# A ring of four buffers for the wide sums of w_ada, and the scan tables' products behind the last h

## The chip, the cores and the metric

The kernel runs on one core of a Trainium2 chip. The metric is the device time of one execution in microseconds, as the median of several runs. Five engines work side by side, each with an instruction queue of its own that it takes in order: TensorE (PE; its weight loads are the profile's PEld), VectorE (DVE), ScalarE (ACT), GpSimd (POOL) and SyncE (SP), which here issues most transfers between HBM and on-chip memory. They wait for one another by semaphores.

## What is computed

One decoder block on 256 positions of width 2048, in float32. A conditioning vector c makes six vectors of scales and shifts through `w_ada` (2048 x 12288, 100 MB). The normalised input, scaled by `sc1` and shifted by `sh1`, is h; h times `w_in` gives the input u of a state-space branch, q, k, v of an attention branch and two gates. A merge, an output projection and an MLP of width 8192 follow. Cut to what matters here:

```python
c_act = jax.nn.silu(c)
mod = c_act @ w_ada[l] + b_ada[l]
sh1, sc1, g1, sh2, sc2, g2 = [m[:, None, :] for m in jnp.split(mod, N_MOD, axis=-1)]
h = rms_norm(x, norm_mix_g[l]) * (1.0 + sc1) + sh1
proj = h @ w_in[l]
u, q, k, v, ga, gb = jnp.split(proj, split_at, axis=-1)
y_ssm = s5_branch(u, ssm_a_re[l], ssm_a_im[l], ssm_log_dt[l], ...)
y_att = moba_attention(q.reshape(shp), k.reshape(shp), v.reshape(shp), rel_bias)
merged = (jax.nn.sigmoid(ga) * (y_ssm @ w_proj_ssm[l])
          + jax.nn.sigmoid(gb) * (y_att @ w_proj_attn[l]))
x = x + g1 * (merged @ w_out[l])
h2 = rms_norm(x, norm_mlp_g[l]) * (1.0 + sc2) + sh2
x = x + g2 * (jnp.square(jax.nn.relu(h2 @ w_ff1[l])) @ w_ff2[l])
```

## The kernel before

**Weight tiles.** Every matrix is read in tiles of 128 rows by 1024 columns (0.5 MB). `load` (L157) puts the transfer on SP's queue, into one of seven buffers `wraw`. `split` makes two halves for the matmuls: ScalarE casts the tile to the high part `whi` (L162), VectorE subtracts that from the tile for the low part `wlo` (L164); each has four buffers. Every product is high x high, high x low and low x high. `gemm_t` (L222 to L224) takes the weights as the stationary operand, in 24 matmuls of 256 columns a tile; `gemm_n` (L275 to L279) takes h as the stationary one, in 12 matmuls of 512 columns.

**The units of w_in.** h comes into being piece by piece, 128 rows ("k tile", kt 0 to 15) or two of them at a time. So the product with `w_in` is cut into units (which, first group, last group): `which` is 0 q, 1 k, 2 v, 3 u, 4 one gate, and the k tiles come in groups of 1, 3, 4 and 8 (kt 0; 1 to 3; 4 to 7; 8 to 15). `qkvu` runs a unit, starts the stream of the next one (`prime`) and moves the sums out of PSUM. Numbered through, unit (0,1,2) has weight tiles 18 to 24, then (1,2,2), (2,2,2), (3,2,2) have four each, (4,2,3) has 37 to 48 (kt 4 to 15), (0,3,3) has 49 to 56, (3,3,3) 57 to 64, (1,3,3) 65 to 72 and (2,3,3) 73 to 80.

**The sums of w_ada.** The first two vectors of `w_ada` (`sc1`, `sh1`) are needed for h. For kt 0 to 3 TensorE sums them (`ada_first`). For kt 4 to 15 VectorE does, in 24 wide sums: `ada_wide` loads 128 rows of 2048 columns (1 MB, two transfers, L375) and multiplies them with silu(c) in one instruction with a running sum (L381). Four sums make two k tiles of h: `hjob` lets ScalarE scale and shift (L514) and splits the result (L162, L164 on `ah`). The buffers of the wide sums lie in `hv` and `hq`, the slots that `bp` ("VT") and `cc` ("QT") of the state-space tables take over later. `ringed` sets which load follows which sum: for the first twelve sums there are four buffers, load i + 4 after sum i; for the last twelve (kt 10 to 15) two buffers, those of `hq`, load i + 2 after sum i.

**Lanes.** Work beside the units is dispatched by lanes: after each weight tile `step` adds a lane's rate to its credit (at most 3) and runs one job for each whole credit. A job's instructions get their place in the program there; a planner with a timeline of its own then sets the order on each engine by priority (weight tiles rank higher by an offset) and dependency.

- Lane `ada`: three empty jobs, the first four loads, two empty jobs, then the 24 sums and 6 `hjob`s, then 97 late jobs (the sums of the other vectors, half as wide, L339). Its rate is R1 = .92; from `hjob(8)` (tile 23) R2; from `hjob(14)` R3 = .15; from the flush on R4 = .5, later rates from 1.0 to .1. So `hjob(14)`, 15 jobs behind `hjob(8)`, would come at .56 on tile 50; `want` (L1139) runs the lane as far as the k tile of the moment needs it, and forces it on tile 47, where kt 14 begins.
- Lane `ssm`: eighteen empty jobs, then the tables of the scan: `ssm_build1` in four parts of six products on VectorE (L676 to L678; the first part into `cmp`, the others into `bp`), `ssm_cc`, `ssm_build3`, transposes on TensorE (`ssm_build2`, L711) and `ssm_build4` (matmuls L748, sums L754), which reads `tt` in slot "T". Rate 1.0, SR1 after unit (0,1,2), SR2 = 1.4 from `hjob(14)`. By the count, five jobs of `ssm_build1` are dispatched ahead of `hjob(14)`.

**After (3,3,3).** `hop_in` copies u into the scan's layout in 32 small transfers on POOL's queue (L853). `flush("ssm")` dispatches what is left of that lane, the `ada` lane goes to R4, `bias_load` loads the attention's bias `tz` into slot "T" in four transfers on POOL's queue (L550), and units (1,3,3) and (2,3,3) follow. Then one gate runs with the attention's jobs (`attn1`, L801 to L813, reads `tz` on VectorE) beside it, and after that the scan.

Of the kernel before, what the change touches and what calls it, by code (L numbers as in the profile page):

```python
# [39 lines left out]
OFF = 300  # L40
HOT = 4000
OF1 = 3000
SR1 = .27
SR2 = 1.4
SC = 1.0
NS = 2
SL = 18
R1 = .92
R2 = .56
R3 = .15  # L50
R4 = .5
RS0 = 1.0
# [25 lines left out]
class Kern:  # L78
# [872 lines left out]
    def body(self):  # L951
# [121 lines left out]
        def seeds(which):  # L1073
            def f(b):
                d, view = views(which, b)
                return lambda o: (view(o), d)
            return [f(b) for b in range(4)]
# [3 lines left out]
        def evac(which, banks, add):  # L1081
            if which == 4 and add:
                self.ga = self.slot("X16", [P, 2, D], name="ga")
            elif which == 4:
                gpart["p"] = self.slot("S4", [P, 2, 1024], name="gp")
            for b in range(4):
                d, view = views(which, b)
                if which == 4 and add:
                    d = self.ga[:, b // 2, (b % 2) * 512:(b % 2) * 512 + 512]
                nc.scalar.copy(d, view(banks[b]))  # L1090
# [23 lines left out]
        def place(which, g0, g1):  # L1114
            return win, range(groups[g0][0], sum(groups[g1])), (1024, 2048, 3072, 0, 4096)[which]

        def qkvu(u, after=None):
            which, g0, g1 = u
            f = self.gemm_n if which in (2, 4) else self.gemm_t
            banks = f(*place(*u), self.ah, self.al, seed=seeds(which) if g0 else None)  # L1120
            if after:
                self.prime(*place(*after))
            evac(which, banks, g0)
# [3 lines left out]
        def hjob(k0):  # L1127
            def f():
# [3 lines left out]
                if k0 == 8:  # L1132
                    self.lanes["ada"][1] = R2
                if k0 == 14:
# [9 lines left out]
        nop = lambda: None  # L1144
        units = []
        wide = [h[:, 2 * i:2 * i + 2, :].rearrange("p k c -> p (k c)") for h in (hv, hq) for i in range(2)]
        ring = wide * 3 + wide[2:4] * 6
        for k0 in range(4, KT, 2):
            units += mod1(k0, 2, ring) + [(None, hjob(k0))]
        free = {None: range(4)}  # L1150
        free.update({i: (i + 4,) for i in range(8)})
        free.update({i: (i + 2,) for i in range(10, 22)})

        def drain(n):
            while len(ready) < n:
# [10 lines left out]
        for u, after in zip(order, order[1:] + [None]):  # L1166
            qkvu(u, after)
            if u == (0, 1, 2):
                self.lanes["ssm"][1] = SR1
        self.want = lambda kt: None  # L1170
        self.hop_in()
        self.flush("ssm")
        self.lanes["ada"][1] = R4
        self.bias_load()
        qkvu((1, 3, 3), (2, 3, 3))
        qkvu((2, 3, 3))
        ga = self.ga
        self.asc = ga[:, :, 1024:1792]
# [389 lines left out]
```

## Time and profile before

| | |
|---|---|
| three runs, median (lowest to highest) | 1390.79 us (1390.17 to 1392.34) |
| the profiled execution | 1391.66 us |
| its span, first to last instruction | 1389.9 us |
| granted clock of TensorE, mean | 0.992 |
| read from HBM | 350.79 MB |
| busy: TensorE, VectorE, ScalarE, GpSimd | 97%, 75%, 55%, 3% |

The profile shows one execution. A time in it counts from the span's first instruction. Rows of the order of time have the start, the duration, the engine, the line, the operation, the tile written and the tiles read; in square brackets stands how long the engine had been idle before, and what ended that. Rows of groups have the number of instructions, the busy time and the mean duration in ns, then the idle time in front of them. "SPq" and "POOL DMA" rows are the issue of a transfer, not the transfer. TensorE's matmuls overlap, so their spacing, not their duration, is the pace.

### The profile page before, as it was taken

The page shows a single profiled execution, that of the slowest core. Times are in us where ns is not written, and L with a number is a line of the kernel's source. Part 1 is how long each engine was busy: PE and PEld are TensorE (multiplying, and loading weights), DVE is VectorE, ACT ScalarE, POOL GpSimd, SP SyncE. Part 2 cuts the span into 40 slices and gives each one's busy share as a digit, 9 for nine tenths or more (in the row PEclk, how much of TensorE's full clock was granted, in tenths as well). Part 3 has the DMA queues.
Part 4 walks back from the last instruction along what each step waited for, and adds up shares of the span by engine and source line. Part 5 has one row for each costly group of instructions (what it writes and reads, how often), then busy time and mean ns, then how long its engine had stood idle before and what let it go on. Part 6 is the DMA issues. An engine that isn't in the chain of part 4 may idle for free.

```text
span 1389.9 us, 21608 instructions
## 1 busy us (share of the span) xinstructions
PE 1354.8 (97%) x8314; PEld 1173.4 (84%) x8314; DVE 1045.5 (75%) x1449; ACT 758.2 (55%) x1052; POOL 42.6 (3%) x96
## 2 busy tenths in 40 slices
PE   7999899999999999999999999999999999999997
PEld 5898789988788897888999888888888888888885
DVE  6798987688797898988885976777666555555676
ACT  6767458456655843446555665444453554634543
POOL 1000001300002200000000000000000000000000
PEclk9999989999999999999999999999999999999999
DMA  9999946898355989898597878798867656566562
GB/s 374 407 396 382 349 150 203 242 326 322 107 172 192 329 291 332 292 387 303 204 355 231 297 242 251 246 255 283 256 232 248 198 188 197 182 193 195 177 199 69
DMA packets 112424, 356.43 MB, mean 256 GB/s; under 512 B 12241, under 2 KB 12273, under 8 KB 111905
## 3 DMA queue, kind: packets, MB, share of 16 engines
q1 hardware_dynamic: 109280, 348.96, 73.0%
q0 software_dynamic: 2896, 5.83, 1.5%
q8 instruction: 65, 1.06, 0.3%
q10 hardware_dynamic: 144, 0.26, 0.1%
q14 instruction: 39, 0.31, 0.1%
HBM read 350.79 MB, written 2.51 MB: 254 GB/s over the span
## 4 chain that ended last, share of the span: by engine, by line
PE 83%; DVE 7%; ACT 4%; DMA 3%; issue 2%; SPq 0%; ACTq 0%; DVEq 0%
PE pn L275 15%; PE pn L277 15%; PE pn L279 15%; PE pd L240 13%; PE pd L244 7%; PE pt L224 5%; PE pt L222 5%; PE pt L223 5%; DVE wlo L164 2%; ACT whi L162 1%; DMA wraw<-in_w_proj_ssm_dram 1%; DVE ahm L381 1%; DVE wraw L339 1%; DMA ahm<-in_wat_dram 1%; PE rk L748 1%
## 5 line engine op out<-in xcount | busy, mean ns | idle before, releaser
L162 ACT CAST whi<-wraw 128x1024 fp32r<-128x1024 f32 x448 | 467.4, 1052 | 511.8 <-PE pn L277 224.7
L164 DVE TENSOR_TENSOR wlo<-wraw,whi 128x1024 fp32r<-128x1024 f32 x448 | 545.0, 1222 | 258.8 <-ACT whi L162 254.6
L240 PE MATMUL pd<-h2h,whi 128*128 128x512 f32 x800 | 208.8, 393 | 0.0
L275 PE MATMUL pn<-whi,ff 128*128 128x512 f32 x496 | 193.0, 389 | 0.0
L277 PE MATMUL pn<-whi,ff 128*128 128x512 f32 x496 | 193.0, 389 | 0.0
L279 PE MATMUL pn<-wlo,ff 128*128 128x512 f32 x496 | 191.6, 389 | 0.0
L240 PEld LDWEIGHTS pd<-h2h,whi 128*128 128x128 f32 x800 | 140.6, 189 | 21.8
L339 DVE SCALAR_TENSOR_TENSOR wraw<-wraw,cb 128x1024 f32<-128x1024 f32 x128 | 155.9, 1218 | 0.0
L275 PE MATMUL pn<-whi,ah 128*128 128x512 f32 x320 | 126.8, 402 | 3.4 <-ACT ah L162 1.5
L277 PE MATMUL pn<-whi,ah 128*128 128x512 f32 x320 | 126.6, 396 | 0.0
L244 PEld LDWEIGHTS pd<-h2h,wlo 128*128 128x128 f32 x800 | 116.0, 190 | 12.4
L244 PE MATMUL pd<-h2h,wlo 128*128 128x256 f32 x800 | 119.2, 282 | 0.0
L279 PE MATMUL pn<-wlo,ah 128*128 128x512 f32 x320 | 117.4, 400 | 0.4 <-DVE wlo L164 0.4
L222 PE MATMUL pt<-ah,whi 128*128 128x256 f32 x384 | 108.9, 290 | 4.3 <-ACT ah L162 3.5
L224 PE MATMUL pt<-ah,wlo 128*128 128x256 f32 x384 | 103.4, 287 | 7.3 <-DVE wlo L164 7.2
L279 PEld LDWEIGHTS pn<-wlo,ff 128*128 128x128 f32 x496 | 93.1, 188 | 19.5
L275 PEld LDWEIGHTS pn<-whi,ff 128*128 128x128 f32 x496 | 93.1, 188 | 19.1
L277 PEld LDWEIGHTS pn<-whi,ff 128*128 128x128 f32 x496 | 93.2, 188 | 19.0
L223 PE MATMUL pt<-ah,whi 128*128 128x256 f32 x384 | 107.8, 285 | 0.0
L222 PEld LDWEIGHTS pt<-ah,whi 128*128 128x128 f32 x384 | 73.8, 193 | 6.5 <-ACT ah L162 3.6
L224 PEld LDWEIGHTS pt<-ah,wlo 128*128 128x128 f32 x384 | 71.7, 194 | 8.2 <-DVE wlo L164 8.1
L275 PEld LDWEIGHTS pn<-whi,ah 128*128 128x128 f32 x320 | 61.0, 191 | 17.6 <-ACT ah L162 2.0
(376 smaller groups left out, 2029.3 us busy)
## 6 DMA issues: line engine op xcount, KB each, us to landing
wraw<-in_w_ff_dram SPq DMA_DIRECT2D x256, 512.0 KB, 4.8
wraw<-in_w_in_dram SPq DMA_DIRECT2D x128, 512.0 KB, 5.9
wraw<-in_wat_dram SPq DMA_DIRECT2D x128, 512.0 KB, 5.7
ahm<-in_wat_dram SPq DMA_DIRECT2D x48, 512.0 KB, 9.9
wraw<-in_w_out_dram SPq DMA_DIRECT2D x32, 512.0 KB, 6.6
wraw<-in_w_proj_attn_dram SPq DMA_DIRECT2D x16, 512.0 KB, 5.8
wraw<-in_w_proj_ssm_dram SPq DMA_DIRECT2D x16, 512.0 KB, 6.5
ahm<-in_wan_dram SPq DMA_DIRECT2D x8, 512.0 KB, 11.4
```

The source lines that it names most:

```text
L162: h = self.nc.scalar.copy(hi, src)
L164: s = self.nc.vector.tensor_sub(lo, src, hi.bitcast(F32))
L222: nc.tensor.matmul(o, hi[:, c], xh[:, kx, :], start=st, stop=False, skip_group_check=True)
L223: nc.tensor.matmul(o, hi[:, c], xl[:, kx, :], start=False, stop=False, skip_group_check=True)
L224: self.mm = nc.tensor.matmul(o, lo[:, c], xh[:, kx, :], start=False, stop=sp, skip_group_check=True)
L240: nc.tensor.matmul(banks[blk], hi[:, cut(blk, k)], x2[:, ks[k], :, :], start=i + k == 0, stop=False, skip_group_check=True)
L244: self.mm = nc.tensor.matmul(banks[blk][:, S:2 * S], lo[:, cut(blk, k)], x2[:, ks[k], 0, :], start=False, stop=last and k == 1, skip_group ...
L275: nc.tensor.matmul(o, xh[:, kx, tk], hi[:, c], start=q == 0 and not full, stop=False, skip_group_check=full)
L277: nc.tensor.matmul(o, xl[:, kx, tk], hi[:, c], start=False, stop=False, skip_group_check=full)
L279: self.mm = last = nc.tensor.matmul(o, xh[:, kx, tk], lo[:, c], start=False, stop=q == n - 1, skip_group_check=full)
L339: v.scalar_tensor_tensor(w, w, 1.0, self.cb[:, (i % 2) * 1024:(i % 2 + 1) * 1024], op0=OP.mult, op1=OP.mult, accum_out=pc[:, i:i + 1])
L381: sm = v.scalar_tensor_tensor(w, w, 1.0, self.cb, op0=OP.mult, op1=OP.mult, accum_out=pc[:, i:i + 1])
```

## The change

Three constants and three places of the order of work. The last twelve wide sums use the same four buffers as the first twelve, load i + 4 after sum i. The `ada` lane runs at .75 jobs a weight tile instead of .56 between `hjob(8)` and `hjob(14)`: by the count, the last wide sum is dispatched on tile 42 and `hjob(14)` on tile 43. The `ssm` lane has rate 0 after unit (0,1,2), so the first `ssm_build1` is dispatched with `hjob(14)`; the last job of the lane falls on tile 65 (it fell on 64). Unit (1,3,3) is moved ahead of `flush("ssm")`, the change to R4 and `bias_load`; its tiles are run with R3, and ten late jobs by the end of (2,3,3) become eight.

```diff
-SR1 = .27
+SR1 = 0.0
...
-R2 = .56
+R2 = .75
...
-        ring = wide * 3 + wide[2:4] * 6
+        ring = wide * 6
...
-        free.update({i: (i + 4,) for i in range(8)})
-        free.update({i: (i + 2,) for i in range(10, 22)})
+        free.update({i: (i + 4,) for i in range(20)})
...
         self.hop_in()
+        qkvu((1, 3, 3), (2, 3, 3))
         self.flush("ssm")
         self.lanes["ada"][1] = R4
         self.bias_load()
-        qkvu((1, 3, 3), (2, 3, 3))
         qkvu((2, 3, 3))
```

## The prediction

> **What bounds the kernel now.** I read the page first, then stretches of the span (the view of windows), then the order of time on TensorE, VectorE and the queues inside the one stretch that stands out.
>
> ```profile
> PE 1354.8 (97%) x8314; PEld 1173.4 (84%) x8314; DVE 1045.5 (75%) x1449; ACT 758.2 (55%) x1052; POOL 42.6 (3%) x96
> ...
> PE   7999899999999999999999999999999999999997
> ...
> PEclk9999989999999999999999999999999999999999
> ```
>
> PE is busy 97% of the span, so an edit can win only where PE stands idle or runs at a lowered clock. The slices show that at the start and the end, which the change doesn't touch, and in the fifth and sixth slices (139 to 208 us), where both rows have an 8. The windows narrow this down; their columns are the stretch, its length, the busy time of each engine, the granted clock, the DMA share and GB/s.
>
> ```profile
> 0.00:100.00 100.00, 87.77 (x766) 77.44 (x766) 76.99 (x177) 70.94 (x113) 4.40 (x19) 0.98 1.00 395
> 100.00:154.00 54.00, 53.08 (x336) 47.66 (x337) 49.44 (x56) 37.29 (x57) 1.31 (x2) 1.00 1.00 366
> 154.00:168.30 14.30, 14.30 (x65) 11.84 (x64) 12.95 (x16) 6.81 (x9) 0.00 (x0) 1.00 1.00 382
> 168.30:175.40 7.10, 0.32 (x3) 0.12 (x1) 5.11 (x7) 0.94 (x1) 0.00 (x0) 0.87 0.61 231
> 175.40:183.80 8.40, 7.78 (x22) 6.34 (x23) 6.39 (x11) 2.94 (x6) 0.00 (x0) 0.50 0.38 125
> 183.80:231.00 47.20, 47.20 (x387) 46.66 (x386) 41.72 (x41) 37.51 (x68) 0.00 (x0) 1.00 0.56 176
> 231.00:340.00 109.00, 109.00 (x823) 95.94 (x823) 84.05 (x134) 60.17 (x103) 17.26 (x36) 1.00 0.87 296
> 340.00:360.00 20.00, 17.41 (x113) 13.69 (x113) 7.75 (x17) 16.11 (x36) 0.11 (x1) 0.91 0.23 79
> ```
>
> From 168.3 to 175.4 PE does nothing, and up to 183.8 it runs at half the clock. Until 168.3 the DMA engines are full (share 1.00); in the hole they are not. PE in order of time:
>
> ```profile
> 168.22 0.28 PE L222 MATMUL pt<-ah,whi 128*128 128x256 f32 x1
> 168.34 0.28 PE L223 MATMUL pt<-ah,whi 128*128 128x256 f32 x1
> 175.48 0.58 PE L224 MATMUL pt<-ah,wlo 128*128 128x256 f32 x1 [6.86 <-DVE wlo L164]
> ```
>
> PE wants the low half of a weight tile (`wlo`), which VectorE has not made yet. VectorE in the same time:
>
> ```profile
> 161.55 2.28 DVE L381 SCALAR_TENSOR_TENSOR ahm<-ahm,cb 128x2048 f32<-128x2048 f32 x1
> ...
> 171.99 2.29 DVE L381 SCALAR_TENSOR_TENSOR ahm<-ahm,cb 128x2048 f32<-128x2048 f32 x1 [1.99 <-DMA ahm<-in_wat_dram]
> 174.21 0.08 DVE L381 DVE_READ_ACCUMULATOR ahm<-ahm,cb 128x1 f32 x1
> 174.21 2.35 DVE L164 TENSOR_TENSOR wlo<-wraw,whi 128x1024 fp32r<-128x1024 f32 x2
> 176.48 0.15 DVE L990 TENSOR_TENSOR B<-pw,cols 128x2 f32<-128x2 f32 x1
> 178.50 0.69 DVE L164 TENSOR_TENSOR ah<-htmp,ah 128x512 fp32r<-128x512 f32 x1 [1.87 <-ACT ah L162]
> ```
>
> The last wide sum stands in VectorE's queue ahead of that low half and waits for its own load; the last h (k tiles 14 and 15) follows, complete at 178.50 + 0.69 = 179.2, and the remaining tiles of unit (4,2,3) had to wait for it. On SP's queue that load was issued late:
>
> ```profile
> 163.87 0.81 SPq L375 DMA_DIRECT2D ahm<-in_wat_dram  x2
> ```
>
> It went out in the moment in which the sum two places before it had ended (161.55 + 2.28 = 163.8): a ring of two buffers. It landed when the sum could begin, at 171.9, eight microseconds later. So the bound here is the ring, then VectorE's order, then PE.
>
> **The stall's price.** These are PE's groups between 168.35 and 183.8:
>
> ```profile
> L279 PE MATMUL pn<-wlo,ah 128*128 128x512 f32 x5 | 2.9, 573 | 0.0
> L277 PE MATMUL pn<-whi,ah 128*128 128x512 f32 x4 | 2.5, 628 | 0.0
> L275 PE MATMUL pn<-whi,ah 128*128 128x512 f32 x4 | 2.1, 669 | 0.5 <-ACT ah L162 0.5
> L224 PE MATMUL pt<-ah,wlo 128*128 128x256 f32 x4 | 1.8, 457 | 6.9 <-DVE wlo L164 6.9
> L223 PE MATMUL pt<-ah,whi 128*128 128x256 f32 x4 | 1.5, 382 | 0.0
> L222 PE MATMUL pt<-ah,whi 128*128 128x256 f32 x4 | 1.5, 381 | 0.0
> ```
>
> One L279 and one L222 of these began before the stretch, which leaves 12 matmuls of 512 columns and 11 of 256. At the full clock a 512-wide one follows the last after 0.227 us (the window from 154 to 168.3 has 63 starts of them in its 14.3 us), a 256-wide one after 0.12 (168.22 to 168.34 above). That is 12 x 0.227 + 11 x 0.12 = 4.0 us of work in 15.5 us: **11.5 us lost**, 7.1 by standing still, 4.4 by the half clock and a short gap before 178.52. This is all that the change can win here; below, it can win nothing.
>
> **Ring and rate.** Counted from the lanes, the last sum is dispatched on weight tile 42 in place of 47, and the last h on 43 in place of 47 (where `want` forces it). PE reaches tile 47 at 168.3. Is h ready by then? Three counts. By bytes: the last load stands behind 24 wide loads (25.2 MB), 16 pieces of the first sums (8.4), 42 weight tiles (22.0), x, the scan's tables and small ones (3.7): 59.3 MB. The windows show 39.5 MB by 100 us and 19.8 more by 154, together 59.3. The queue had moved as many bytes at 154; only their order changes. Sum 2.3, then 4.9 us from the sum's end to h (174.28 to 179.2): **h at about 161**. By VectorE's work:
>
> ```profile
> L164 DVE TENSOR_TENSOR wlo<-wraw,whi 128x1024 fp32r<-128x1024 f32 x26 | 30.8, 1216 | 0.0
> L381 DVE SCALAR_TENSOR_TENSOR ahm<-ahm,cb 128x2048 f32<-128x2048 f32 x12 | 27.4, 2284 | 4.3 <-DMA ahm<-in_wat_dram 4.3
> ...
> L676 DVE TENSOR_TENSOR tt<-cmp,AB 128x512 f32<-128x512 f32 x2 | 1.3, 681 | 0.0
> ```
>
> (groups of VectorE from 100 to 170 us). From in front of h go ten products of 0.68 (the first table's six and four of the next: 6.8 us), waits for wide loads (4.3 in these rows and the 1.99 at 171.99) and four low halves of 1.2 (4.8), since h stands four tiles earlier: 17.9 us, so again 161. By PE: that is 7 us ahead of need. I take the stall as gone, -11.5; the other end is 0.
>
> What may be late next is VectorE before 168, where the sums are now packed closer: twelve from tile 25 to 42. PE takes 2.88 us for a transposed tile (24 x 0.12) and 2.72 for a straight one, 50 us for these 18. VectorE's part is 18 x 1.2 + 12 x 2.3 + three splits of 0.69 and small ones, about 52.
>
> ```profile
> 105.50:168.30 62.80, 62.22 (x361) 54.55 (x360) 56.89 (x64) 41.80 (x62) 0.75 (x2) 1.00 1.00 371
> ```
>
> Over the whole stretch it fits: 56.9 - 6.8 (products) + 5.3 (two sums and a split that came after 168.3) = 55.4 of 62.8. But in the bunch it is 2 us over, with the lead of a few low halves as cover. Bounds 0 and +4 (twice that excess); I take +0.5.
>
> A rule of the Trainium skill speaks against the ring: the page "DMA: Bandwidth & Descriptors", section "Specifications", puts the limit of one core's HBM traffic at about 358 GB/s (further down it has 425 measured for one core streaming alone). By it the 59.3 MB alone would need 166 us, an estimate that would put h near 173 and leave most of the stall. The row from 0 to 100 us has 395 GB/s, so the measurement decides against the rule here, and the sum goes by the row.
>
> **Products behind the last h.** They are the same 6.8 us on VectorE, later. Where do they fit? From 168.3 to 231 VectorE was busy 5.11 + 6.39 + 41.72 = 53.2 of 62.7 us. Afterwards the stretch has 11.5 us less, 51.2, for 53.2 + 6.8 - 5.3 = 54.7. So 3.5 us don't fit and spill behind unit (3,3,3). There the next row has 25 us idle in 109, and since the flush now follows unit (1,3,3), nothing forces them in front of its eight tiles. Cover gone, they would cost 3.5, and at most all of their 6.8; no gain is possible, as PE is full there. I take +1, since the queue is in order and a product of 1.2 us in front of a low half can make PE wait a little.
>
> **The unit in front of the flush.** Its matmuls and the products' on PE are the same, in another order: 0. The `ada` lane runs these eight tiles at .15 instead of .5: by the end of unit (2,3,3) eight late jobs are dispatched, not ten. Each of the two is half a wide sum (some 1.2 us of VectorE) and one load, and moves into later lanes; by their rates 99 of the 97 jobs there are would be dispatched before the flush at L1505 (101 before), so none is left for it: 0. On POOL's queue `bias_load` still follows the 32 copies of `hop_in`:
>
> ```profile
> 239.87 6.74 DVE L754 SCALAR_TENSOR_TENSOR rt<-rk,rmask,rt 128x512 f32<-128x512 f32 x12
> ```
>
> ```profile
> 257.67 0.49 POOL L853 DMA_DIRECT2D u<-uT  x1 [0.55 <-DMA u<-uT]
> 258.24 1.95 POOL L550 DMA_DIRECT2D tz<-scr  x4
> ```
>
> ```profile
> 269.63 0.40 DVE L804 SCALAR_TENSOR_TENSOR ga<-sco,tz 128x128 f32<-128x128 f32 x1 [0.23 <-PE sco L802]
> ```
>
> The slot of `tz` comes free at 246.6 with the last product; the copies end at 257.7. So the copies, whose place doesn't change, set the load, with 11 us to spare: 0. The stall of the attention's end (window 340 to 360: 2.6 us idle, and 9% of 20 us of clock, 1.8) may grow or go with the order of the jobs: bounds -4.4 and +4.4, taken at 0.
>
> One rule prices new small waits. The Trainium skill, "TensorE: Matmul & The Clock Gate", section "HAM oscillation — how this bites in real kernels", asks only that PE have no gap over about 3.4 us. Here the clock fell in the 340 to 360 row, whose idle 2.6 us is under that; by the rule a few waits of 1 us cost themselves alone (-10.0 below), by the row they may cost 1.8 us more.
>
> Sum: -11.5 + 0.5 + 1 = -10.0, and +0.5 for such a lowered clock: **-9.5**. The profiled execution took 1391.66 (span 1389.9); that gives 1382.2, and 0.9 less on the median of 1390.79: **1381.3 us**.
>
> **Rivals.**
> 1. *VectorE becomes the bound* (sums bunched, products without cover): -11.5 + 4 + 3.5 = -4, 1386.8. For it: 52 against 50 us, 54.7 against 51.2. Against: the whole stretches have room.
> 2. *The transfers are the bound.* The loads only stand earlier in a full queue. At the 296 GB/s of the row from 231 to 340 the last 19.8 MB would take 67 us, landing at 167, h at 174: five earlier than before. PE then idles 174 - 168.3 = 5.7 us and pays 1.8 for a lowered window as in the 340 row; -11.5 + 7.5 = -4, 1387. Against: share 1.00 went with 366 to 395. The Trainium skill's limit of 358 GB/s, named above, belongs to this rival.
> 3. *Nothing comes of it*: each engine's instructions stand in an order planned ahead, not in the program's. If the plan keeps products or low halves behind the last sum, PE waits as long elsewhere: 1390.8.
> 4. *Slower: `tz` late.* If the last product, now allowed a unit later, ends eight tiles later, the slot comes free up to 23 us later (8 x 2.88) against PE. VectorE's in-order queue then holds at L804, and low halves wait behind; four are made ahead, 10.9 us of cover. PE loses 23 - 10.9 + 5 of half clock = 17: 1398. It decides from 18 us of lateness on, where it eats the gain. For it: L804 ran 0.2 us after its last wait. Against: the 11 us to spare, and the last product is dispatched only one tile later.
>
> **How the numbers follow.** Forecast 63%, rival 1 16%, rival 2 5%, rival 3 11%, rival 4 5%. The forecast's own spread goes from 1378 (all 11.5, a little of the attention's stall) to 1385. With rivals 1 and 2 the range reaches to 1388; it leaves out rivals 3 and 4 and a tail below, some 18%. Faster by over 0.2% (2.8 us, about what a measurement tells from no change) holds in the forecast and rivals 1 and 2: 84%; same 11%, slower 5%.
>
> **What would show it.** In the profile after: no PE gap over 2 us and no lowered clock between 100 and 240 us; no wide sum that waits for its load; the last h near 161; products of `cmp` and `bp` all behind it; unit (3,3,3) ending about 11 us earlier. The prediction is wrong if TensorE's wait for `wlo` is as long as before, if h comes after 168, or if L804 waits for a DMA.

## The result and the profile after

| | before | after |
|---|---|---|
| median of the compared runs (4 each) | 1391.57 us | 1381.52 us |
| lowest to highest | 1390.17 to 1393.39 | 1379.81 to 1382.28 |
| the profiled execution | 1391.66 | 1382.28 |
| its span, granted clock | 1389.9, 0.992 | 1380.5, 0.996 |

The ratio after to before is 0.9925, with a 95% interval of 0.9908 to 0.9943: some 10 us faster, 0.2 us from the predicted 1381.3. But the sum came out so well partly by luck, since its errors cancelled, and the cause given for the stall was the wrong one.

The title names the ring and the products; the third part of the change, the `ada` lane's rate of .75, turned out to carry the most.

The page of the kernel after, its busy times and two rows of the 40 slices:

```profile
PE 1351.3 (98%) x8314; PEld 1171.1 (85%) x8314; DVE 1044.6 (76%) x1449; ACT 757.5 (55%) x1052; POOL 42.7 (3%) x96
...
PE   6999999999999999999999999999999999999997
...
PEclk9999999999999999999999999999999999999999
```

The 8 of the fifth and sixth slices is gone. The windows of the kernel after (columns as in the prediction) show what replaced it:

```profile
100.00:168.00 68.00, 65.17 (x386) 57.05 (x386) 57.83 (x65) 42.20 (x64) 1.32 (x2) 0.97 0.93 356
168.00:184.00 16.00, 15.48 (x85) 13.35 (x84) 15.96 (x20) 12.05 (x18) 0.00 (x0) 1.00 0.83 265
184.00:290.00 106.00, 104.57 (x957) 99.22 (x956) 84.70 (x109) 67.19 (x113) 17.30 (x36) 1.00 0.69 217
290.00:360.00 70.00, 69.36 (x438) 57.67 (x437) 54.18 (x91) 45.73 (x88) 0.11 (x1) 1.00 0.72 247
```

and the same stretches before:

```profile
100.00:168.00 68.00, 67.08 (x398) 59.24 (x398) 62.09 (x71) 43.99 (x64) 1.31 (x2) 1.00 1.00 370
168.00:184.00 16.00, 8.60 (x27) 6.90 (x26) 11.96 (x17) 4.19 (x7) 0.00 (x0) 0.68 0.49 174
184.00:290.00 106.00, 106.00 (x973) 100.81 (x971) 83.41 (x105) 69.22 (x116) 17.26 (x36) 1.00 0.71 219
290.00:360.00 70.00, 67.41 (x349) 55.28 (x349) 49.94 (x86) 44.37 (x90) 0.11 (x1) 0.98 0.73 271
```

In the second stretch TensorE now starts 85 matmuls instead of 27, at the full clock. In the first it starts 12 fewer and idles 2.83 us instead of 0.92; in the third it idles 1.43 us where it idled 0; in the fourth it gains 1.95 and the clock.

**Where the time went.** The same matmul (the n-th of its line and tiles) can be looked up in two traces. The table says how much later it begins than in the kernel before, as the median over the 20 us from there on; below zero is ahead. Each row is one execution: those of `e_prod`, `k_rate27` and `j_ring2` were the fastest of their runs (`e_prod`'s by 3.4 us against its median), those of `g_r66`, `d_move` and `n_after` the slowest. The value that each execution has at 100 us, where the order of work is still the same (+1.45 in the kernel after), is taken off; it comes from the first transfers.

| kernel | 160 us | 200 | 260 | 360 | 500 | 1300 |
|---|---|---|---|---|---|---|
| after | +3.9 | -7.6 | -5.4 | -9.5 | -10.5 | -10.8 |
| after, second profile (n_after) | +3.9 | -7.6 | -5.8 | -10.0 | -9.9 | -9.4 |
| a_ring | +1.8 | -3.1 | +2.3 | -2.5 | -2.2 | -1.4 |
| b_rate | +4.3 | -7.5 | -6.0 | -10.2 | -12.1 | -10.9 |
| b_rate, second profile (n_rate) | +6.3 | -5.5 | -3.3 | -7.6 | -9.1 | -7.4 |
| k_rate27 | +7.5 | -2.3 | -3.0 | -7.3 | -8.8 | -8.5 |
| e_prod | -0.5 | -5.2 | -1.3 | -6.2 | -7.4 | -5.9 |
| j_ring2 | +4.8 | -6.7 | -5.1 | -9.2 | -10.8 | -9.0 |
| g_r66 | +2.2 | -9.5 | -8.0 | -12.2 | -12.2 | -5.9 |
| c_nomove | +2.4 | -9.0 | -7.1 | -11.3 | -12.0 | -5.8 |
| o_late75 | +2.4 | -9.0 | -7.4 | -11.5 | -9.4 | -10.1 |
| m_late66 | +2.2 | -9.5 | -8.0 | -12.2 | -9.8 | -8.1 |
| d_move | 0.0 | -1.1 | -1.1 | +2.6 | +6.6 | +7.6 |

For the kernel after: 3.9 us lost before the stall's place, 11.5 won there (from +3.9 to -7.6), 2.2 given back up to 260, 4.1 won up to 360, 0.9 from there to 500 and 0.3 after that. With the +1.45 of the start that leaves -9.4, the difference of the spans. Its VectorE in order of time, around the last sum:

```profile
159.73 2.28 DVE L381 SCALAR_TENSOR_TENSOR ahm<-ahm,cb 128x2048 f32<-128x2048 f32 x1
161.94 0.08 DVE L381 DVE_READ_ACCUMULATOR ahm<-ahm,cb 128x1 f32 x1
161.94 1.22 DVE L164 TENSOR_TENSOR wlo<-wraw,whi 128x1024 fp32r<-128x1024 f32 x1
163.08 2.28 DVE L381 SCALAR_TENSOR_TENSOR ahm<-ahm,cb 128x2048 f32<-128x2048 f32 x1
...
165.51 1.22 DVE L164 TENSOR_TENSOR wlo<-wraw,whi 128x1024 fp32r<-128x1024 f32 x1
167.67 1.23 DVE L164 TENSOR_TENSOR wlo<-wraw,whi 128x1024 fp32r<-128x1024 f32 x1 [0.93 <-ACT whi L162]
168.82 0.68 DVE L164 TENSOR_TENSOR ah<-htmp,ah 128x512 fp32r<-128x512 f32 x1
169.42 0.68 DVE L676 TENSOR_TENSOR tt<-cmp,fr 128x512 f32<-128x512 f32 x1
```

and of its groups from 100 to 170 us the wide sums, of SP's queue the last wide load:

```profile
L381 DVE SCALAR_TENSOR_TENSOR ahm<-ahm,cb 128x2048 f32<-128x2048 f32 x14 | 32.0, 2285 | 0.0
```

```profile
143.57 0.86 SPq L375 DMA_DIRECT2D ahm<-in_wat_dram  x2
```

No sum waits for its load any more (0.0 us of idle in front of all 14). The last load is issued by 144.4; with the median of 7.3 us to landing that the transfers' view has for these loads between 140 and 156 us, it is there at about 152. Its sum begins only at 163.08, 11 us later. The last h is complete at 168.82 + 0.68 = 169.5, TensorE takes the tile that needs it (47) at 173.6, and the first product of the tables follows h at 169.42.

### The profile page after: what moved, and what is told of

Read it like the earlier page. It is cut to its first block, busy times and chain, and to the rows that moved or that the text cites. A ratio compares the mean times of both kernels' runs of the same rounds, so it can differ in the third digit from the quotient of the medians.

```text
span 1380.5 us, 21609 instructions
## 1 busy us (share of the span) xinstructions
PE 1351.3 (98%) x8314; PEld 1171.1 (85%) x8314; DVE 1044.6 (76%) x1449; ACT 757.5 (55%) x1052; POOL 42.7 (3%) x96
## 4 chain that ended last, share of the span: by engine, by line
PE 89%; DVE 4%; ACT 3%; DMA 3%; issue 1%; SPq 0%; DVEq 0%; ACTq 0%
PE pn L275 17%; PE pn L277 17%; PE pn L279 17%; PE pd L240 13%; PE pd L244 7%; PE pt L222 5%; PE pt L224 5%; PE pt L223 5%; DMA ahm<-in_wat_dram 1%; DVE wlo L164 1%; ACT whi L162 1%; DVE ahm L381 1%; PE ys L933 1%; DMA wraw<-in_w_in_dram 0%; DMA xt<-in_xt_dram 0%
## 5 line engine op out<-in xcount | busy, mean ns | idle before, releaser
L279 PE MATMUL pn<-wlo,ah 128*128 128x512 f32 x320 | 113.7, 393 | 0.0
L222 PEld LDWEIGHTS pt<-ah,whi 128*128 128x128 f32 x384 | 74.7, 196 | 7.8 <-ACT ah L162 3.3
L223 PEld LDWEIGHTS pt<-ah,whi 128*128 128x128 f32 x384 | 75.0, 195 | 0.4 <-issue 0.2
## 6 DMA issues: line engine op xcount, KB each, us to landing
ahm<-in_wat_dram SPq DMA_DIRECT2D x48, 512.0 KB, 10.1
ahm<-in_wan_dram SPq DMA_DIRECT2D x8, 512.0 KB, 10.2
```

What stands on the lines that cost most here:

```text
L222: nc.tensor.matmul(o, hi[:, c], xh[:, kx, :], start=st, stop=False, skip_group_check=True)
L223: nc.tensor.matmul(o, hi[:, c], xl[:, kx, :], start=False, stop=False, skip_group_check=True)
L279: self.mm = last = nc.tensor.matmul(o, xh[:, kx, tk], lo[:, c], start=False, stop=q == n - 1, skip_group_check=full)
```

## The experiments

Two theories stood at the outset. By the one, which is the prediction's, the ring of two made the last load, and so the stall. By the other the ring was a symptom: a sum stood late because its job was dispatched late (by `want`, on tile 47), behind low halves and products, and an earlier load would have lain there waiting. All ratios are to the kernel before on the same chip.

**The ring without the rate.** The ring of four, and the products behind h, at the old rate and without the move (the ring by itself, with the products in front of h, was not run):

```diff
-SR1 = .27
+SR1 = 0.0
-        ring = wide * 3 + wide[2:4] * 6
+        ring = wide * 6
-        free.update({i: (i + 4,) for i in range(8)})
-        free.update({i: (i + 2,) for i in range(10, 22)})
+        free.update({i: (i + 4,) for i in range(20)})
```

> The kernel before with the ring of four and the products behind the last h (SR1 = 0); rate .56 and the flush stay. Theory (the ring cleared the stall, the rate brought the last h in front of TensorE's need): no wide sum waits for its load any more, but the last two sums are dispatched together on tile 47, and 2 x 2.3 us of sums and 4.9 us to h stand behind that; about 4 us of TensorE's 7.1 us stall remain, 1386 us. Rival A (the rate alone cleared it): stall as before, 1390 to 1392. Rival B (ring and products are the whole of it): 1381 to 1383.

Measured: 1391.73 us, ratio 0.9990 (0.9979 to 1.0000). VectorE, in order of time:

```profile
170.25 2.29 DVE L381 SCALAR_TENSOR_TENSOR ahm<-ahm,cb 128x2048 f32<-128x2048 f32 x1
...
172.53 3.49 DVE L164 TENSOR_TENSOR wlo<-wraw,whi 128x1024 fp32r<-128x1024 f32 x3
175.94 0.15 DVE L990 TENSOR_TENSOR B<-pw,cols 128x2 f32<-128x2 f32 x1
177.90 0.69 DVE L164 TENSOR_TENSOR ah<-htmp,ah 128x512 fp32r<-128x512 f32 x1 [1.81 <-ACT ah L162]
```

TensorE, in order of time, and the window:

```profile
174.94 0.39 PE L224 MATMUL pt<-ah,wlo 128*128 128x256 f32 x1 [2.81 <-DVE wlo L164]
```

```profile
168.00:184.00 16.00, 12.20 (x46) 9.55 (x45) 13.96 (x20) 5.86 (x8) 0.00 (x0) 0.79 0.51 163
```

The sums wait for no load here either, and the last sum still begins at 170.25 and h still comes at 178.6 (before: 171.99 and 179.2). The hole is smaller (46 matmuls against 27), but the 4.9 us that the table has for it between 160 and 200 are what `e_prod` below wins there, 4.7, with no ring. So the ring isn't what bounds. The theory put on record for this run was right about what stays of the hole (some 4 us; TensorE idles 3.8 in this window) and wrong about the time, 1386: by 260 us the table has 5.4 us given back.

**The rate without the ring.** `R2` = .75 and `SR1` = 0, with the old ring of two and without the move:

```diff
-SR1 = .27
+SR1 = 0.0
-R2 = .56
+R2 = .75
```

> The kernel before with rate .75 and the products behind the last h (SR1 = 0); the ring of two and the flush stay. Theory: with two buffers a load goes out only when the sum two places before it has ended and lands 7 to 8 us later, so sums that are dispatched closer together wait in VectorE's queue for their loads, low halves behind them; over 6 us of waits for wide loads on VectorE, TensorE's gaps no smaller in sum, 1390 to 1400 us. Rival A (the rate alone cleared the stall): 1381 to 1384.

Measured: 1382.47 us, 0.9935 (0.9914 to 0.9957). The groups of VectorE from 100 to 180 us, VectorE in order of time, and the window:

```profile
L381 DVE SCALAR_TENSOR_TENSOR ahm<-ahm,cb 128x2048 f32<-128x2048 f32 x14 | 32.0, 2287 | 9.6 <-DMA ahm<-in_wat_dram 9.6
```

```profile
164.21 2.29 DVE L381 SCALAR_TENSOR_TENSOR ahm<-ahm,cb 128x2048 f32<-128x2048 f32 x1 [0.56 <-DMA ahm<-in_wat_dram]
...
173.53 0.69 DVE L164 TENSOR_TENSOR ah<-htmp,ah 128x512 fp32r<-128x512 f32 x1
```

```profile
168.00:184.00 16.00, 16.00 (x88) 13.84 (x88) 15.49 (x20) 11.53 (x18) 0.00 (x0) 1.00 0.80 264
```

The sums wait 9.6 us for their loads, more than before the change, and TensorE doesn't idle at all in the stall's place. The last sum begins at 164.2 with two buffers and at 163.1 with four. The theory on record had the waits right and their price wrong: they cost TensorE no hole, and the time is Rival A's. Nearly the whole gain comes from two numbers.

**The whole change with the ring of two.** The counterpart:

```diff
-        ring = wide * 6
+        ring = wide * 3 + wide[2:4] * 6
-        free.update({i: (i + 4,) for i in range(20)})
+        free.update({i: (i + 4,) for i in range(8)})
+        free.update({i: (i + 2,) for i in range(10, 22)})
```

> The changed kernel with the ring of two put back. Theory Q (the ring does nothing for the time, as .56 with four buffers was no faster and .75 with two was): within 2 us of the changed kernel, 1380 to 1383.5, with 5 to 10 us of waits for wide loads on VectorE that cost TensorE nothing. Rival (the ring is worth something beside the move): 1385 or above.

Measured: 1384.97 us, 0.9940 (0.9925 to 0.9955). The sums wait 10.2 us for loads, h comes at 173.5, and there is no hole. The time lies between the two forecasts. With the ring the ratio is 0.9925: it may be worth some 2 us, but the intervals overlap.

**The products alone.** `SR1` = 0 and nothing else:

```diff
-SR1 = .27
+SR1 = 0.0
```

> The kernel before with the products behind the last h (SR1 = 0) alone: ring of two, rate .56, flush as before. With the ring of four as well, the attention's stall at 345 was gone, as it was in every kernel with SR1 = 0 and in none with .27. Theory P (SR1 = 0 gives the planner another order, which clears that stall; the hole at 168 comes from the late dispatch of the last sums and stays): hole near 170 of 5 to 8 us, no stall at 345, some 4 us given back between 100 and 240; 1389 to 1392 us. Rival: the hole is gone too once VectorE is rid of 6.8 us of products, 1381 to 1384.

Measured: 1388.72 us, 0.9961 (0.9947 to 0.9975). TensorE in order of time, and a window:

```profile
171.68 0.58 PE L224 MATMUL pt<-ah,wlo 128*128 128x256 f32 x1 [4.00 <-DVE wlo L164]
```

```profile
240.00:260.00 20.00, 17.53 (x328) 16.66 (x327) 15.54 (x27) 8.80 (x14) 10.36 (x22) 1.00 0.84 235
```

Ten products out of VectorE's way let h come 3.9 us earlier (175.3) and shrink the hole from 6.86 to 4.00, a gain of 4.7 us up to 200 us in the table. Then 3.9 are given back by 260: TensorE, which was never idle from 184 to 290 before, stands 2.5 us here, while the tables' sums (`rt`, L754) end at 254.3 instead of 246.6. So the hole stays, as Theory P said, though it is under the 5 us that it named.

**The rate without the products.** `R2` = .75, `SR1` stays .27:

```diff
-R2 = .56
+R2 = .75
```

> The kernel before with rate .75 alone: ring of two, SR1 = .27, flush as before. Theory Q (the rate alone clears the hole at 168, since the last two sums are dispatched on tiles 41 and 42 and not together on 47; products stay in front): no gap over 3 us from 160 to 185, the attention's stall of 5 us stays; 1383 to 1387. Rival (it needs the products out of VectorE's way): the bunched sums and four to five products make TensorE wait 5 us and more, 1389 or above.

Measured: 1385.00 us, 0.9944 (0.9929 to 0.9959). Here the loss ahead of the stall's place is the largest, 7.5 us, with a lowered clock of 3.4 us after 122: low halves, sums and products are all packed there. The hole left is under 2 us:

```profile
169.89 1.19 PE L279 MATMUL pn<-wlo,ah 128*128 128x512 f32 x4 [1.59 <-DVE wlo L164]
```

What is given back by 260 is nothing: the products were done early. Theory Q was right about the hole and the time, and wrong about the attention's stall, which is gone (-3.0 to -7.3 in the table). Only this rate differs from the kernel before here, and the sums still wait 8.1 us for loads from 100 to 180 us. So the rate carries most of the gain, and the rate `SR1` = 0 shifts a cost from before 168 to after 200.

**The move alone.**

```diff
+        qkvu((1, 3, 3), (2, 3, 3))
         self.flush("ssm")
         self.lanes["ada"][1] = R4
         self.bias_load()
-        qkvu((1, 3, 3), (2, 3, 3))
         qkvu((2, 3, 3))
```

> The kernel before with nothing but the move of unit (1,3,3) in front of the flush. Theory M (the move clears the attention's stall): the 7 us hole at 168 stays, the one at 345 goes, 1386 to 1388. Rival (the move does nothing there): 1391.

Measured: 1396.12 us, 1.0019 (1.0006 to 1.0031): slower by some 3 us, which neither forecast had. The hole stays (6.01 us of idle at 173.34), and TensorE has a new gap, while ScalarE moves v out of PSUM:

```profile
292.02 0.50 PE L275 MATMUL pn<-whi,ah 128*128 128x512 f32 x1 [2.60 <-ACT v L1090]
```

**Everything but the move.** Unit (1,3,3) back behind the flush:

```diff
-        qkvu((1, 3, 3), (2, 3, 3))
         self.flush("ssm")
         self.lanes["ada"][1] = R4
         self.bias_load()
+        qkvu((1, 3, 3), (2, 3, 3))
```

> The changed kernel with unit (1,3,3) put back behind the flush. In the changed kernel TensorE is 3.9 us ahead at the end of unit (2,3,3) and 8.1 behind the gate's unit: the stall at the end of the attention is gone, which the prediction had put at 0. Theory M (the move did that, by letting the attention's first scores and softmax through earlier): the stall of some 3 us and a lowered clock at 340 come back, 1385 to 1386. Rival (it came from the earlier start of the whole, or the rates): no stall there, 1381 to 1382.

Measured: 1385.91 us, 0.9954 (0.9940 to 0.9968). The time is the one that Theory M gave, but not for its reason: the stall at 340 doesn't come back (one gap of 0.42 us there). Up to 500 us it is ahead of the kernel after (-12.0 against -10.5), and loses the lead after that: from 500 to 560 us TensorE is busy 56.29 us at a mean clock of 0.97, in the kernel after 59.90 at the full clock. This kernel and the next lose their lead in the same place, so I asked what they have in common.

**A lower rate.** `R2` = .66 in the kernel after, to bunch the sums less:

```diff
-R2 = .75
+R2 = .66
```

> The changed kernel with rate .66 instead of .75: the last sum falls on tile 44 in place of 42, h on 46 in place of 43. The changed kernel lost 3.9 us between 100 and 165 to sums in front of low halves, with one clock window at half speed at 133. Theory B (the loss is from the bunching of 12 sums in 18 tiles): 1.5 to 3 us of it come back and h is still in time for tile 47 or 2 us late: 1379 to 1381. Rival (h now comes too late, as at .56): a gap of 3 us and more near 170, 1384 to 1390.

Measured: 1385.50 us, 0.9946 (0.9929 to 0.9962). The bunch costs 2.2 us instead of 3.9, no sum waits for a load, h comes at 170.1, and at 360 us it leads the kernel after by 2.7 us. Then it loses over 6 us from 500 on. So the time is the rival's without the rival's cause: near 170 no gap is longer than 0.3 us. The waits from 500 to 560 us (total, times, longest), here and in the kernel after:

```profile
ACT whi L162 <- DMA wraw<-in_w_proj_ssm_dram: 19.9, 9, 6.1
```

```profile
ACT whi L162 <- DMA wraw<-in_w_proj_ssm_dram: 13.5, 8, 5.4
```

ScalarE's casts wait longer for the weight tiles of the state-space branch's projection. An obvious theory: the kernel that arrives earlier meets transfers that can't be earlier, because the late jobs (0.5 MB each) share them. Two kernels took load away there by the `ada` lane's later rates, `RPA` from .69 to .62 and `RS2` from .35 to .5, one at `R2` = .66 and one at .75.

```diff
-R2 = .75
+R2 = .66
-RS2 = .35
+RS2 = .5
-RPA = .69
+RPA = .62
```

> The changed kernel with rate .66, and the late w_ada jobs moved from 32 weight tiles where the DMA engines are full (RPA .69 to .62, 2.2 jobs fewer) to the 16 of the gate's last unit, where they are not (RS2 .35 to .5, 2.4 more). With .66 alone TensorE was 2.7 us further ahead after the attention than in the changed kernel and lost 6 us from 517 to 550 and near 675, where ScalarE waited for weight tiles. Theory D (late loads share the queue with the weight tiles there; fewer of them keep the lead): 1378 to 1381 in the numbers of a chip where the kernel before takes 1391, ratio 0.990 to 0.992, faster than both. Rival (that place is TensorE's arrival against something else than late loads): as .66 alone, 0.994 to 0.996.

Measured: 1384.37 us, 0.9938 (0.9926 to 0.9951). TensorE is busy 58.59 us of the 60 from 500 to 560 instead of 56.59, but 2.4 us are lost before 500: half a confirmation (the ratio lies between the two forecasts), and no better kernel.

```diff
-RS2 = .35
+RS2 = .5
-RPA = .69
+RPA = .62
```

> The changed kernel (rate .75) with the same shift of late jobs alone. The changed kernel lost nothing at 517 to 550. Theory D: nothing to win there, within 1.5 us of the changed kernel. Rival (the new place of the jobs, beside the scan's products on VectorE, costs more): 2 us slower or more.

Measured: 1381.89 us, 0.9921 (0.9908 to 0.9933), the same as the kernel after within both intervals. Its program equals that kernel's up to some 300 us, which makes it a second look at the bunch (below).

**The change again, and the rate without the ring again**, with more runs on one chip. The kernel after, unchanged:

> The changed kernel itself, beside the three others of this call on one chip. All theories: 0.992 to 0.994 of the kernel before.

and `b_rate`, unchanged:

> Rate .75 and SR1 = 0 with the ring of two and the flush as before (the second of the first four, again). Theory Q (ring and move are worth nothing, rate and products are the change's whole gain): within 2 us of the changed kernel, 0.992 to 0.995. Rival (ring or move carry a part): 3 us or more slower than it.

Measured: 1381.82 us, 0.9924 (0.9911 to 0.9937), and 1384.01 us, 0.9940 (0.9927 to 0.9953). The ring and the move together are worth 2.2 us by the medians, between the two forecasts; the intervals overlap, but four of the five runs of the kernel after are below all five of `b_rate`. With the move, the ring's kernels are ahead (0.9925 against `j_ring2`'s 0.9940); without it they are behind (`c_nomove`'s 0.9954 against `b_rate`'s 0.9935). So what the ring is worth by itself, some 2 us either way, stays open. No kernel run here is clearly faster than the one with the change.

## Why the prediction was right, and where it was not

**What bounds: TensorE's hole, its price.** Right. By the count of the matmuls in it the stall was worth 11.5 us, and from 160 to 200 us TensorE gains 11.5.

**"So the bound here is the ring": this step failed.** The trace had a wait of 1.99 us for a load, a ring of two behind that load, and a hole right after; I read them as one chain. `a_ring` removes the wait, and the hole is left about as `e_prod` leaves it without the ring; `b_rate` and `j_ring2` wait 9.6 and 10.2 us for loads, where the kernel before waited 6.3 (the prediction's 4.3 and 1.99), and have no hole. What bounded was the place of the last sums in VectorE's order: their jobs were dispatched on tile 47, and with the rate they are dispatched five tiles earlier, while products go behind h. The change contains both, so the forecast of the stall held all the same. Had the change been the ring and the products at the old rate, the same argument would have promised 11 us for the 0.1% of `a_ring`.

**h at about 161.** Wrong by 8.5 us: 169.5. The count by bytes was right (the last load was to land at 154, it came at about 152), but the counts took h to follow the load. A sum dispatched on tile 42 stands behind low halves that wait for ScalarE's casts, and these for TensorE to give back a buffer: 0.93 us at 167.67 in the rows above, and of the waits from 100 to 175 us (total, times, longest):

```profile
DVE wlo L164 <- ACT whi L162: 8.4, 5, 3.8
ACT whi L162 <- PE pt L223: 7.6, 4, 2.5
```

So the low halves keep VectorE to TensorE's pace, and in the planned order the sums stand between them. Of the 7 us of lead that I counted on, 4.1 were left (169.5 to 173.6). By the words of the prediction, h after 168 would have proved it wrong. That condition was too strict: the need itself came later, too, because of the next term. Of the prediction's other signs, three came true (no gap over 2 us, no sum that waits for its load, the products behind h) and two did not: the clock fell once between 100 and 240 us, and the last sums of unit (3,3,3) left PSUM 7.5 us earlier, not 11 (the last copy to `uT` begins at 231.03 instead of 238.58).

**The bunch: +0.5 predicted, bounds 0 and +4; it cost 3.9.** The value I chose lay at the wrong end, and the reason (packed closer than VectorE can run, so that low halves come late) isn't shown. Of the 3.9, about 1.5 are a lowered clock, since `o_late75` and `c_nomove`, with the same sums in the same place but no lowered clock, lose 2.4. TensorE's waits from 100 to 168 us (total, times, longest) name mostly ScalarE, which copies earlier sums into PSUM (L206), and low halves less:

```profile
PE pt L222 <- ACT pt L206: 1.2, 1, 1.2
PE pn L275 <- ACT pn L206: 0.8, 3, 0.3
PE pt L224 <- DVE wlo L164: 0.7, 3, 0.4
```

Before, these were 0.5 for L206 and 0.4 for low halves; in `b_rate` 3.4 and 0.4. What holds the copies up stays open. Nor is it the rate alone: with the ring of four the loss is 1.8 at .56 (`a_ring`), 2.2 at .66 and 2.4 at .75; with the ring of two at .75 it is 4.3 (`b_rate`) and 4.8 (`j_ring2`), all at the full clock. Rival 1 had the price, +4, but VectorE as the bound isn't what these rows show.

**Products behind h: +1 predicted, bounds 0 and 6.8; 2.2 given back.** The spill was right and mis-sized. (The prediction's "product of 1.2 us" was two of them: its own row has 0.68 each.) All four tables' sums end at 248.5 in the kernel after, 1.9 us later than before although TensorE is six ahead at 200, and TensorE waits for them, as its order of time shows:

```profile
243.40 0.68 PE L748 MATMUL rk<-cc,tt 64*64 64x64 f32 x16 [1.00 <-DVE rt L754]
```

The comparison of `k_rate27` (products early, nothing given back), `b_rate` (1.5) and `e_prod` (3.9) supports it. I had overlooked that TensorE's own matmuls of the tables use these products, so that late products needn't push low halves to cost time.

**The unit in front of the flush, `tz`: 0.** Right for `tz`: the load went out on POOL's queue at 251.60 and L804 ran at 265.34 with no wait for it, so Rival 4 is out. The rest is open: with the full change the move costs nothing that shows; alone it costs 3 us.

**The attention's end: 0 predicted, bounds ±4.4; 4.1 won.** Before, TensorE's order of time had three gaps there:

```profile
346.64 0.84 PE L820 MATMUL ptr<-ident,ga 128*128 128x128 f32 x3 [0.46 <-ACT ga L812]
348.26 0.70 PE L828 MATMUL pav<-ga,v 128*128 128x256 f32 x2 [0.78 <-ACT ga L821]
350.45 0.50 PE L275 MATMUL pn<-whi,ah 128*128 128x512 f32 x1 [1.27 <-ACT ga L1213]
```

2.5 us, and a lowered clock behind them. After, one is left:

```profile
344.33 0.50 PE L275 MATMUL pn<-whi,ah 128*128 128x512 f32 x1 [0.64 <-ACT ga L1212]
```

This gain isn't the move's (`c_nomove` has it without, `d_move` has the move and not the gain), nor the ring's (`e_prod` and `k_rate27` have it without). `SR1` = 0 by itself brings it (`e_prod`), and so does `R2` = .75 by itself (`k_rate27`). Every kernel with another rate in either lane has it. The attention's instructions are the same and stand in another planned order. What in the planner decides was not found; it stays open.

**The lowered clock, +0.5.** Right that it can come from gaps which are each short (1.24 and 0.36 us); it came in the bunch, not in the attention.

**The sum.** Predicted -11.5 + 0.5 + 1 + 0.5 = -9.5. Measured, in the same order: -11.5 + 3.9 + 2.2, then -4.1 at the attention's end, +1.45 at the start, and -1.3 from 360 on: -9.4. The bunch and the products were taken 4.6 us too cheap, and a gain of 4.1 that I had put at zero paid for them. The range had these bounds in it, and so held; that the point was 0.2 us off is luck.

Rival 2 fell: share and GB/s stayed high (356 GB/s from 100 to 168 us, with 406 to 411 in the first five rows of the last section), and the loads landed when the byte count said. The Trainium skill's 358 GB/s for a core ("DMA: Bandwidth & Descriptors", section "Specifications") is passed by some 50 in those rows. Rival 3 fell for the whole change, but `a_ring` is very nearly what it described: the plan keeps low halves ahead of h, and 0.9990 comes of it.

## What to carry to other kernels

A wait for a load that is named in front of a late instruction doesn't show that the load bounds it: ask when the job was dispatched and what stands ahead of it on its own engine, and if that would have kept it there anyway, move the dispatch and not the buffer. Packing side work closer in front of a need costs the main engine in small gaps, and pushing other work behind the need costs where its results are used; both were a few microseconds here, up to a third of the stall's price, so neither should be set near zero. In a kernel whose order a planner makes, small edits shift stalls of some 4 us far away in either direction; a range for such a change has to hold them.

## What the hardware showed that I had not expected

A lowered clock after two short gaps. In the kernel after, TensorE idles 1.24 us in front of 131.71 and 0.36 in front of 132.57, and then runs at half the clock for 3.4 us. In `o_late75`, whose program is the same up to there, it idles 1.24 us in front of 131.04 and 0.37 in front of 131.92, and the clock stays full.

The stretches of one granted clock last multiples of 3.413 us in the traces, all but the last of each (in the kernel after 105.81 at full clock, 31 times that, and then 3.41 at half), so it looks as if the clock were set anew in steps of 3.413 us. Here are windows cut at these steps, in the kernel after:

```profile
129.87:133.28 3.41, 1.81 (x12) 1.37 (x11) 2.79 (x4) 3.41 (x7) 0.00 (x0) 1.00 1.03 410
133.28:136.70 3.42, 3.42 (x19) 3.42 (x18) 3.42 (x4) 3.28 (x5) 0.00 (x0) 0.50 1.03 410
```

in `o_late75`:

```profile
127.47:130.88 3.41, 2.34 (x12) 1.78 (x10) 3.06 (x4) 2.27 (x5) 0.00 (x0) 1.00 1.03 410
130.88:134.29 3.41, 2.88 (x21) 2.67 (x22) 2.79 (x3) 3.41 (x7) 0.00 (x0) 1.00 1.02 406
134.29:137.70 3.41, 3.41 (x31) 3.41 (x30) 3.38 (x6) 2.55 (x3) 0.00 (x0) 1.00 1.04 411
```

and in `d_move`, around its gap of 2.60 us in front of 292.02:

```profile
287.15:290.57 3.42, 2.28 (x12) 1.44 (x10) 2.56 (x7) 1.23 (x4) 0.00 (x0) 1.00 0.99 339
290.57:293.98 3.41, 1.96 (x9) 1.62 (x10) 2.44 (x4) 3.41 (x7) 0.00 (x0) 1.00 1.03 420
293.98:297.39 3.41, 3.41 (x17) 2.82 (x16) 0.17 (x1) 1.00 (x3) 0.00 (x0) 1.00 0.92 322
```

In the kernel after both gaps lie in one step, 1.60 us of idle, and the next step has 19 matmuls at half the clock. In `o_late75` a step's edge cuts the same idle time into 1.07 and 0.53, in `d_move` the 2.60 into 1.14 and 1.45, and the clock stays full. In the 14 traces, from 30 to 1365 us, half the clock follows all ten steps at full clock with 1.60 us of idle or more and none with less than 1.41; in between both occur. So the section "HAM oscillation — how this bites in real kernels" of the Trainium skill's page "TensorE: Matmul & The Clock Gate", which warns of gaps over about 3.4 us, doesn't cover this case. In these traces the idle time within one step counts, and two executions of the same instructions can fall on either side, since the steps fall in other places of the kernel.
